# Two-layer decoder trunk on one core: partial sums moved ahead of the first evaluations, a transposition of x placed later and copied out by two engines

## The chip, the cores and the metric

The kernel runs on one core of one Trainium2 chip. The metric is device time in microseconds (us) of one execution. The core has a matrix engine (TensorE, PE in the profile, with its weight loads as PEld), a vector engine (VectorE, DVE), a scalar or activation engine (ScalarE, ACT), a general engine (GpSimd, POOL) and a sync engine (SyncE, SP). Each has its own instruction queue. Matmul results land in PSUM and are taken out by DVE or ACT; DMAs here are issued by SP and POOL.

## The reference

Two layers, each of three sub-layers with a normalisation before and after it. The input x is 512 tokens by 1024; all numbers are float32.

```python
for l in range(DEPTH):                       # DEPTH = 2
    gn = norm_gains[l]
    h = rms_norm(x, gn[0])
    x = x + 0.5 * rms_norm(swiglu(h, w_ffn1_gate[l], w_ffn1_up[l], w_ffn1_down[l]), gn[1])
    h = rms_norm(x, gn[2])
    ...                                      # mixer: gated recurrence and windowed attention
    x = x + rms_norm(mixed @ w_out[l], gn[3])
    h = rms_norm(x, gn[4])
    x = x + 0.5 * rms_norm(swiglu(h, w_ffn2_gate[l], w_ffn2_up[l], w_ffn2_down[l]), gn[5])

def swiglu(h, w_gate, w_up, w_down):         # hidden width 2816 = 22 blocks of 128
    return (jax.nn.silu(h @ w_gate) * (h @ w_up)) @ w_down
```

The change touches the four feed-forward stages (`swiglu` with its norms), not the mixer.

## The kernel before

**Number format.** Every float32 product is done as three matmuls in a rounded format: an operand is split into a high part (an ACT cast) and a low part (DVE: the number less its high part), and `mm3` (matmuls at L103) adds high·high, high·low and low·high.

**Weights.** `Stream` holds the weights' order as a list of items, one block of 128 x 1024 each. `split` (L191) makes an item's two parts: `whi` by an ACT cast (L219), `wlo` in one of two ways by the item's kind. Kinds "u", "b", "c" use DVE (L226). Kinds "v", "a", "d" use ACT for the negated number (L223) and then a DMA from POOL that adds the raw weight in flight (L224). Raw blocks come through four buffers of tag `w32`, loaded by SP (L187); a buffer is free again when its last reader is done. Six buffers each hold `whi` and `wlo`.

**A feed-forward stage** (`ffn`, L695). The first four of the gate and up blocks are made by `quad`, one accumulator (`acc`, five in all) for each. Then come pairs (gate, up) made by `twice`, 48 matmuls of 256 columns each, or in the very first stage by `project`. `gated` evaluates a pair: ACT's silu of the gate block (L706, into tile z), DVE's product with the up block (L707, into tile u). In the first stage `gated` first multiplies by the row factor rb (L701 to L704). With PLAIN = 4 (first stage FIRST = 6) pairs made that way, the remaining ones go through `fast` (L653).

**fast** computes a gate and an up block for both halves of the tokens with seven products instead of eight, in the manner of Strassen. A product is 12 matmuls of 256 columns. Products 1 and 2, the first two, use parts that are there already; the others use sums of quarters of the operand, `x56` and `x37`. `sums()` makes these for k and k + 4 at a time, so that four calls are needed. A call is, in the stages that are not the first (`Halves.sums`): four DVE additions (L496), four DVE operations in `quarter_sums` (L344 to L347), and two splits (ACT L294, DVE L295). In the first stage (`First.sums`) L411 scales x in place first, and three more splits follow. A call allocates eight tiles of tag s; that tag has 53 slots, and z and u of `gated` are of the same tag.

**Order.** PE runs in the order of the program (`manual_schedule`). For the other engines the framework's list scheduler decides the order ahead of time, with the place in the program as priority; on the chip each queue runs in the order it was given. Side work of PE is interleaved by hand: `Order` keeps a planned clock `order.t` that each matmul advances by an assumed cost, and generators (`spawn`) yield the planned ns until their next step. `order.poll()`, after each block of a matmul group, runs what is due; `order.until(cond)` runs the side work that is due next, back to back, until the condition holds.

**lay** (L394) is one such generator: it transposes x into `x_all`, 8 groups of four PE transposes (L110) through PSUM tiles of tag `aux` (three in all), each copied out by ACT (L401). It is due `WAIT["lay"]` after the start of the planned clock's side work, with `WAIT["laid"]` between groups. The first stage waits for it with `order.until(lambda: pre.laid)` after its sixth projection, since the sums overwrite x. `finish` makes rb, `gain_rows` lays out the gains; both are generators too.

Of the kernel before, what the change touches and what calls it, by code (L numbers as in the profile page):

```python
# [29 lines left out]
SLOTS = 53  # L30

WAIT = dict(
    early=0.0, first=0.0, spread=2750.0, squares=1700.0, lay=30000.0, laid=1000.0, normed=6300.0, final=2600.0,
    head=2600.0, diag=500.0, level=3000.0, chunks=1700.0, blocks=1200.0, norm=4500.0, gate=4500.0,
    values=1200.0, scores=1500.0, exp=16000.0, turn=1600.0, out=1500.0, pair=4000.0, att0=1260.0, att1=10800.0,
)
# [5 lines left out]
def trunk(ctx: ExitStack, tc: tile.TileContext, xin, wall, gains, lbT, hgain, sinks, c_dist, c_mask, c_ident, out):  # L42
    nc = tc.nc
# [15 lines left out]
    def big(dt=F32, shape=None):  # L59
        return sb.tile(shape or [P, S], dt, tag="s", name=nm("s"), bufs=SLOTS)  # L60
# [4 lines left out]
    def acc():  # L65
        return ps.tile([P, S], F32, tag="acc", name=nm("acc"), bufs=5)

    def aux():
        return ps.tile([P, S], F32, tag="aux", name=nm("aux"), bufs=3)
# [39 lines left out]
    def transpose(o, src):  # L109
        nc.tensor.transpose(o, src, ident)  # L110
        order.t += 107.0
# [3 lines left out]
    xt = [[x_all[:, t, h * S : (h + 1) * S] for h in range(2)] for t in range(TT)]  # L115
# [11 lines left out]
    p = aux()  # L127
# [144 lines left out]
    ws = Stream()  # L272
# [7 lines left out]
    def wmm(o, b, mv, start, stop, poll=True):  # L280

        mm3(o, b[2:], mv, start, stop)
        ws.used(b)
        if poll:
            order.poll()
# [76 lines left out]
    class First(Quarters):  # L362
# [31 lines left out]
        def lay(self):  # L394

            for t in range(TT):
                for h in range(2):
                    p = aux()
                    for k in range(4):
                        transpose(p[:, k * P : (k + 1) * P], xs[4 * h + k][:, t * P : (t + 1) * P])  # L400
                    nc.scalar.copy(xt[t][h], p)  # L401
                    yield WAIT["laid"]
            self.laid = True

# [200 lines left out]
    def of_half(pre, k, half):  # L605
        h = pre.h[k]
        if isinstance(pre, Halves):
            return [h[half][:, i, :] for i in range(2)]
        return h if half is None else cut(h, HALF[half])

    def quad(pre, halves):

        o = [acc() for _ in range(4)]
        blocks = {}
        ws.pinned = halves
        for half in (0, 1) if halves else (None,):
            c = WHOLE if half is None else HALF[half]
            for k in range(KT):
                order.until(lambda: pre.have[half or 0] > k)
                for j in range(4):  # L620
                    if (k, j) not in blocks:
                        blocks[k, j] = ws.next(uses=2 if halves else 1)
                    wmm(o[j][:, c], blocks[k, j], of_half(pre, k, half), k == 0, k == KT - 1)
            ws.pinned = False
        return o

    def twice(pre):

        o = acc()
        blocks = [ws.next(uses=2) for _ in range(KT)]  # L630
        for half in (0, 1):
            for k in range(KT):
                wmm(o[:, HALF[half]], blocks[k], of_half(pre, k, half), k == 0, k == KT - 1)
        return o

    def project(pre):
        o = acc()
        for k in range(KT):
            wmm(o, ws.next(), pre.h[k], k == 0, k == KT - 1)
        return o  # L640
# [12 lines left out]
    def fast(pre, a, start):  # L653

        def product(o, it, c, n):
            for k in range(4):
                wmm(o, ws.block(it, c + k), X[n][k], k == 0, k == 3)

        X = {n: pre.operand(n) for n in range(1, 8)}
        H2 = S // 2
        for j in range(start, FT):
            p1, p26, p57, p43 = acc()[:, :H2], acc(), acc(), aux()
            s, v, z = big()[:, :H2], big(F32, [P, 2, H2]), big(F32, [P, 2, H2])

            m = sb.tile([P, 4, H2], F32, tag="m", name=nm("m"), bufs=1)
            w = ws.whole()
            product(p1, w, 0, 1)
            nc.scalar.copy(s, p1)  # L670
            product(p26[:, :H2], w, 4, 2)
            if j == FT - 1:
                for i in range(EARLY):
                    a[i] = split(a[i])
            w = ws.whole()
            product(p57[:, :H2], w, 0, 5)
            product(p57[:, H2:], w, 4, 7)
            c = ws.whole()
            product(p26[:, H2:], c, 0, 6)
            pairs = [p.rearrange("p (i t) -> p i t", i=2) for p in (p26, p57, p43)]  # L680

            nc.vector.tensor_tensor(m[:, 0:4:2, :], pairs[0], s.unsqueeze(1).to_broadcast([P, 2, H2]), op=ALU.add)

            nc.vector.tensor_tensor(v, pairs[1], m[:, 2:3, :].to_broadcast([P, 2, H2]), op=ALU.add)
            w = ws.whole()
            product(p43[:, H2:], w, 4, 3)
            product(p43[:, :H2], c, 4, 4)

            nc.vector.tensor_tensor(m[:, 3, :], p57[:, :H2], v[:, 1, :], op=ALU.add)
            nc.vector.tensor_tensor(m[:, 1:3, :], pairs[2], v[:, ::-1, :], op=ALU.add)  # L690
            nc.scalar.activation(out=m[:, 0:2, :], in_=m[:, 0:2, :], func=AF.Silu)
            nc.vector.scalar_tensor_tensor(z, m[:, 0:2, :], -1.0, m[:, 2:4, :], op0=ALU.mult, op1=ALU.mult)
            a.append(z.rearrange("p i t -> p (i t)"))

    def ffn(l, n, pre, nxt, halves=True):  # L695
        a = []

        def gated(og, ou):
            z, u = big(), big()
            if first:  # L700
                nc.vector.tensor_tensor(z, og, pre.rb, op=ALU.mult)  # L701
                nc.scalar.activation(out=z, in_=z, func=AF.Silu)
                nc.vector.tensor_tensor(u, ou, pre.rb, op=ALU.mult)
                nc.vector.tensor_tensor(u, u, z, op=ALU.mult)  # L704
            else:
                nc.scalar.activation(out=z, in_=og, func=AF.Silu)  # L706
                nc.vector.tensor_tensor(u, ou, z, op=ALU.mult)  # L707
            a.append(u)

        first = isinstance(pre, First)  # L710
        o = quad(pre, halves)
        if first:
            o.append(project(pre))
            order.until(lambda: pre.rb is not None)
        for j in range(2):
            gated(o[2 * j], o[2 * j + 1])
        if first:
            gated(o[4], project(pre))
            order.until(lambda: pre.laid)
            for j in range(3, FIRST):  # L720
                for _ in range(2 if j == 5 else 1):
                    pre.sums()
                gated(project(pre), project(pre))
            fast(pre, a, FIRST)
        else:
            for j in range(2, PLAIN):
                gated(twice(pre), twice(pre))
                pre.sums()
                pre.sums()
            fast(pre, a, PLAIN)  # L730
        return down(a, FT, l, n + 1, nxt)

# [309 lines left out]
    for l in range(DEPTH):  # L1042
        for n in (0, 2, 4):
            if n == 2:
                ws.plain((4 * H + 4 + 2 + 2 * KT) * KT // 8 + 2 * KT * 4 // 8)
                ws.rows(KT)
            else:
                p = FIRST if l + n == 0 else PLAIN
                ws.plain(6)
                ws.plain(2 * p - 6, "v" if l + n == 0 else "u")  # L1050
                ws.pairs(FT - p)
                ws.rows(FT)
    pre = First()
# [65 lines left out]
    for l in range(DEPTH):  # L1119
        pre = ffn(l, 0, pre, (l, 2), halves=l > 0)  # L1120
        pre = mixer(l, pre, (l, 4))
        pre = ffn(l, 4, pre, (l + 1, 0) if l + 1 < DEPTH else None)
# [81 lines left out]
```

## Time and profile before

| | |
|---|---|
| runs | 2213.29, 2214.19, 2214.93 us; median 2214.19 |
| profiled execution | 2213.53 us, span 2211.8 us |
| busy | PE 2172.0, DVE 1366.2, ACT 1046.4, POOL 125.9 us |
| mean granted clock of PE | 0.991 |
| HBM read, written | 200.99 MB, 2.15 MB |

The span is the time from the first to the last instruction that the profile records; the execution's own time is 1.7 us longer. A name such as "L294" is a line of the kernel; "s<-acc" means that a tile of tag s is written from one of tag acc; "x8" is a count. A row of the timeline has start, length, engine, line, operation, tiles, count, and in brackets how long the engine stood idle before it and what released it. Matmul rows overlap, so that the distance of their starts is what counts.

The four feed-forward stages begin, roughly, at 0, 742, 1104 and 1840 us; the first mixer lies between the first and the second of them, the second mixer between the third and the fourth.

### The profile page before, as it was taken

How to read it: one execution, taken by the hardware profiler on the slowest of the kernel's cores; microseconds unless marked ns; L12 is line 12 of the kernel's file. 1: busy time of each engine (PE TensorE's matmuls, PEld its weight loads, DVE VectorE, ACT ScalarE, POOL GpSimd, SP SyncE). 2: the span in 40 equal slices, each digit the busy share in tenths (PEclk: the TensorE clock that was granted, in tenths of full speed). 3: DMA queues.
4: the chain of work that ended last, by engine and by line, in shares of the span. 5: the costliest groups of instructions: out<-in, count | busy, mean ns of one | idle time of the engine just before them, and what ended most of it. 6: DMA issues, size and time to landing. Idle time of an engine off the chain costs nothing.

```text
span 2211.8 us, 34593 instructions
## 1 busy us (share of the span) xinstructions
PE 2172.0 (98%) x13625; PEld 1958.7 (89%) x13625; DVE 1366.2 (62%) x2375; ACT 1046.4 (47%) x1709; POOL 125.9 (6%) x150
## 2 busy tenths in 40 slices
PE   9999999999999989999999999999999999899998
PEld 7999988878888989998899998898788889899987
DVE  5778725756633667883476786267565437777823
ACT  7555515455423545562445555253543335455612
POOL 0111000000000011100001110000000000111000
PEclk9999999999999999999999999999999999999999
DMA  8577532212233238773236775322112322578631
GB/s 241 125 180 185 169 99 74 86 58 66 69 101 99 87 92 185 183 200 96 76 101 148 177 185 163 95 86 67 58 58 86 96 96 77 118 178 186 188 94 39
DMA packets 126419, 263.60 MB, mean 119 GB/s; under 512 B 13392, under 2 KB 71216, under 8 KB 126256
## 3 DMA queue, kind: packets, MB, share of 16 engines
q1 hardware_dynamic: 105088, 203.13, 29.1%
q0 software_dynamic: 21024, 58.21, 15.2%
q8 instruction: 107, 1.75, 0.3%
q14 instruction: 56, 0.46, 0.1%
q10 hardware_dynamic: 144, 0.05, 0.0%
HBM read 200.99 MB, written 2.15 MB: 92 GB/s over the span
## 4 chain that ended last, share of the span: by engine, by line
PE 93%; DVE 4%; DMA 1%; ACT 1%; issue 1%; SPq 0%; DVEq 0%; ACTq 0%; POOLq 0%
PE acc L103 68%; PE aux L103 23%; PE aux L110 1%; DMA w<-wall 1%; PE acc L110 1%; DVE wlo L226 0%; DVE s L496 0%; DVE s L295 0%; DVE s L768 0%; DMA s<-xin 0%; DVE s L453 0%; DVE s L937 0%; ACT whi L219 0%; DMA wlo<-w 0%; DMA g_sb<-gains 0%
## 5 line engine op out<-in xcount | busy, mean ns | idle before, releaser
L103 PE MATMUL acc<-s,whi 128*128 128x256 f32 (+1 forms) x5104 | 1106.2, 313 | 23.7 <-ACT s L294 16.3
L103 PEld LDWEIGHTS acc<-s,whi 128*128 128x128 f32 x5104 | 839.0, 192 | 73.2 <-ACT s L294 17.8
L103 PE MATMUL acc<-s,wlo 128*128 128x256 f32 (+1 forms) x2552 | 794.2, 311 | 0.1
L219 ACT CAST whi<-w 128x1024 fp32r<-128x1024 f32 (+1 forms) x373 | 360.7, 969 | 673.0 <-PE aux L103 276.8
L226 DVE TENSOR_TENSOR wlo<-w,whi 128x1024 fp32r<-128x1024 f32 (+1 forms) x227 | 276.1, 1218 | 407.8 <-ACT whi L219 403.9
L103 PEld LDWEIGHTS acc<-s,wlo 128*128 128x128 f32 x2552 | 490.6, 192 | 26.3 <-DVE wlo L226 0.4
L103 PE MATMUL acc<-whi,s 128*128 128x512 f32 x1296 | 424.2, 393 | 0.0
L103 PEld LDWEIGHTS acc<-whi,s 128*128 128x128 f32 x1296 | 243.3, 188 | 50.9
L103 PE MATMUL acc<-wlo,s 128*128 128x512 f32 x648 | 252.5, 390 | 0.0
L224 POOL DMA_DIRECT2D wlo<-w x146 | 125.7, 861 | 1942.7 <-ACT wlo L223 1790.1
L103 PE MATMUL aux<-whi,s 128*128 128x512 f32 x624 | 207.8, 390 | 0.0
L103 PE MATMUL aux<-s,whi 128*128 128x256 f32 x1120 | 204.6, 283 | 0.0
L226 DVE TENSOR_TENSOR wlo<-tt,whi 128x1024 fp32r<-128x1024 f32 x140 | 170.5, 1218 | 12.8 <-ACT whi L219 12.7
L103 PEld LDWEIGHTS aux<-s,whi 128*128 128x128 f32 x1120 | 174.7, 192 | 0.0
L219 ACT CAST whi<-tt 128x1024 fp32r<-128x1024 f32 x140 | 145.8, 1041 | 31.0 <-PE acc L103 20.8
L103 PE MATMUL aux<-s,wlo 128*128 128x256 f32 x560 | 158.5, 283 | 0.0
L103 PEld LDWEIGHTS acc<-wlo,s 128*128 128x128 f32 x648 | 121.8, 188 | 23.8
L103 PEld LDWEIGHTS aux<-whi,s 128*128 128x128 f32 x624 | 117.2, 188 | 24.1
L206 DVE TENSOR_TENSOR tt<-w,w 128x512 f32<-128x512 f32 x70 | 48.4, 691 | 133.4 <-DMA w<-wall 118.4
L223 ACT ACTIVATE wlo<-w 128x1024 fp32r<-128x1024 f32 (+1 forms) x146 | 124.1, 850 | 0.0
L103 PE MATMUL aux<-wlo,s 128*128 128x512 f32 x312 | 121.4, 389 | 0.0
L103 PEld LDWEIGHTS aux<-s,wlo 128*128 128x128 f32 x560 | 107.5, 192 | 0.0
(163 smaller groups left out, 1889.0 us busy)
## 6 DMA issues: line engine op xcount, KB each, us to landing
w<-wall SPq DMA_DIRECT2D x283, 512.0 KB, 3.5
w<-wall SPq DMA_DIRECT2D x352, 128.0 KB, 2.6
wlo<-w POOLq DMA_DIRECT2D x76, 512.0 KB, 5.9
wlo<-w POOLq DMA_DIRECT2D x70, 256.0 KB, 4.2
grow<-rows_d SPq DMA_DIRECT2D x6, 512.0 KB, 5.0
s<-xin SPq DMA_DIRECT2D x8, 256.0 KB, 6.5
y<-s SPq DMA_DIRECT2D x8, 256.0 KB, 2.5
w<-wall SPq DMA_DIRECT2D x2, 256.0 KB, 4.3
```

The source lines that it names most:

```text
L103: nc.tensor.matmul(o, lhsT, rhs, start=start, stop=stop)
L110: nc.tensor.transpose(o, src, ident)
L206: nc.vector.tensor_tensor(self.t13[:, h[0]], w[:, h[0]], v[:, h[0]], op=ALU.add)
L219: i = nc.scalar.copy(it.hi[:, c], w[:, c])
L223: nc.scalar.mul(it.lo[:, c], w[:, c], -1.0)
L224: nc.gpsimd.dma_start(it.lo[:, c].bitcast(F32), w[:, c], accum_op=ALU.add)
L226: nc.vector.tensor_tensor(it.lo[:, c], w[:, c], it.hi[:, c].bitcast(F32), op=ALU.subtract)
```

## The change

Four edits. In the stages that are not the first, two calls of `sums()` stand ahead of the first `gated`, one ahead of each of the two following pairs; before, two followed each of these pairs. `lay` becomes due at 32000 instead of 30000 planned ns, with 1500 instead of 1000 between groups. Its copies alternate between ACT (h = 0) and DVE (h = 1). In the list of weights, the first eight blocks instead of six of each feed-forward stage are of kind "u"; the remaining ones among the plain blocks are "v". As the stages with PLAIN = 4 have eight plain blocks, all "u" before too, this alters two blocks of the first stage only.

```diff
-    early=0.0, first=0.0, spread=2750.0, squares=1700.0, lay=30000.0, laid=1000.0, normed=6300.0, final=2600.0,
+    early=0.0, first=0.0, spread=2750.0, squares=1700.0, lay=32000.0, laid=1500.0, normed=6300.0, final=2600.0,
...
                     for k in range(4):
                         transpose(p[:, k * P : (k + 1) * P], xs[4 * h + k][:, t * P : (t + 1) * P])
-                    nc.scalar.copy(xt[t][h], p)
+                    (nc.vector.tensor_copy if h else nc.scalar.copy)(xt[t][h], p)
                     yield WAIT["laid"]
...
             o.append(project(pre))
             order.until(lambda: pre.rb is not None)
+        if not first:
+            pre.sums()
+            pre.sums()
         for j in range(2):
             gated(o[2 * j], o[2 * j + 1])
...
             for j in range(2, PLAIN):
+                if j < 4:
+                    pre.sums()
                 gated(twice(pre), twice(pre))
-                pre.sums()
-                pre.sums()
             fast(pre, a, PLAIN)
...
                 p = FIRST if l + n == 0 else PLAIN
-                ws.plain(6)
-                ws.plain(2 * p - 6, "v" if l + n == 0 else "u")
+                ws.plain(8)
+                ws.plain(2 * p - 8, "v")
                 ws.pairs(FT - p)
                 ws.rows(FT)
```

## Prediction

> **What bounds the kernel now.** I read the busy times first, then what TensorE (PE) waited for, then the matmuls around the longest waits, and last the queues of VectorE (DVE) and ScalarE (ACT) at those places. The first line is from the page, the others from the list of waits of PE; there the columns are us in total, times, longest.
>
> ```profile
> PE 2172.0 (98%) x13625; PEld 1958.7 (89%) x13625; DVE 1366.2 (62%) x2375; ACT 1046.4 (47%) x1709; POOL 125.9 (6%) x150
> PE acc L103 <- ACT s L294: 16.3, 6, 4.1
> PE acc L103 <- DVE s L295: 5.8, 6, 1.6
> PE aux L110 <- ACT x_all L401: 2.5, 2, 1.7
> ```
>
> PE is busy for 98% of the span, so only two things can shorten it: fewer waits, or fewer matmuls at a lowered clock. The two longest waits are for L294 and L295, the ACT cast and the DVE subtraction that end each `sums()`. They come six times each, two in each of the three feed-forward stages that are not the first; the third, 2.5 us, is for `lay` (L401) in the first stage.
>
> The stage table prices the three. The rows are, for the stage at 742 us, the stretch before `fast`, its first product group (j=4) and its second; then the first group of the other two stages. The columns are length, then busy time of PE, PEld, DVE, ACT, POOL, then PE's clock, DMA share, GB/s.
>
> ```profile
> 751.43:790.32 38.89, 38.89 (x326) 38.89 (x326) 24.20 (x44) 17.13 (x26) 2.58 (x3) 1.00 0.43 114
> 790.32:810.97 20.65, 13.30 (x86) 12.32 (x86) 15.03 (x30) 7.42 (x11) 0.86 (x1) 0.75 0.18 42
> 810.97:821.05 10.08, 10.08 (x86) 10.08 (x86) 8.05 (x11) 5.94 (x9) 1.72 (x2) 1.00 0.68 171
> 1151.76:1172.57 20.81, 13.47 (x86) 12.48 (x86) 15.03 (x30) 7.42 (x11) 0.86 (x1) 0.75 0.17 41
> 1888.65:1909.63 20.98, 13.54 (x86) 12.55 (x86) 15.03 (x30) 7.42 (x11) 0.86 (x1) 0.76 0.12 31
> ```
>
> A group is 7 products of 12 matmuls, 84 in all, and takes 10.08 us (0.12 us a matmul). The first of each stage takes 20.65, 20.81 and 20.98 us. Just before, 38.89 us pass without a PE gap. So each stage loses 10.57, 10.73 and 10.90 us there: 32.2 us. About 7.3 of each is waiting (16.3 + 5.8 over three); the remaining 3.3 is matmuls at a granted clock of 0.75 instead of 1.00 and short gaps.
>
> Why are the sums late? DVE's order in the stage at 742 us, from the timeline (start, length):
>
> ```profile
> 752.88 2.43 DVE L484 SCALAR_TENSOR_TENSOR s<-aux,g_sb,s 128x256 fp32r<-128x256 f32 x6
> 768.25 0.69 DVE L707 TENSOR_TENSOR s<-acc,s 128x512 f32<-128x512 f32 x1 [4.52 <-ACT s L706]
> 770.92 0.68 DVE L206 TENSOR_TENSOR tt<-w,w 128x512 f32<-128x512 f32 x1
> 778.89 0.69 DVE L707 TENSOR_TENSOR s<-acc,s 128x512 f32<-128x512 f32 x1 [2.15 <-PE acc L103]
> 779.50 1.42 DVE L496 TENSOR_TENSOR s<-s 128x256 f32<-128x256 f32 x4
> 783.95 1.42 DVE L496 TENSOR_TENSOR s<-s 128x256 f32<-128x256 f32 x4
> 790.41 0.69 DVE L707 TENSOR_TENSOR s<-acc,s 128x512 f32<-128x512 f32 x1 [1.93 <-PE acc L103]
> 791.02 1.42 DVE L496 TENSOR_TENSOR s<-s 128x256 f32<-128x256 f32 x4
> 798.38 1.42 DVE L496 TENSOR_TENSOR s<-s 128x256 f32<-128x256 f32 x4
> 802.26 1.51 DVE L295 TENSOR_TENSOR s<-s,s 128x512 fp32r<-128x512 f32 x2
> ```
>
> Two sums follow the third evaluation (L707 at 778.89) at once, two the fourth (790.41). The last pair thus starts when PE is already at `fast`, and its last L295 runs at 802.26, 12 us after PE began the group. Yet the inputs (L484, 752.88 + 2.43) were there at 755.3. What holds a sum is not the data but its place: its tiles have the tag s, as those of the evaluations before it, and L206, which has other tiles and stands still later in the program, ran at 770.92, ahead of it. I conclude that tiles of one tag are given out in program order. This is an inference from the order of the rows.
>
> **The change part by part.**
>
> *Sums moved, three stages.* Nothing is added: four sums before, four after (12 in the kernel), with the same instructions and no DMA; no queue of SP or POOL is passed. Two now stand ahead of the first evaluation, one after the second, one after the third. The first two can start at 755.3. A sum takes 783.95 − 779.50 = 4.45 us of DVE, two 8.9. These rows show the first two evaluations on ACT and the rest of a sum:
>
> ```profile
> 767.62 0.60 ACT L706 ACTIVATE s<-acc 128x512 f32<-128x512 f32 x1
> 782.08 1.14 ACT L294 CAST s<-s 128x512 fp32r<-128x512 f32 x2 [2.19 <-DVE s L345]
> 786.54 1.14 ACT L294 CAST s<-s 128x512 fp32r<-128x512 f32 x2
> L226 DVE TENSOR_TENSOR wlo<-w,whi 128x1024 fp32r<-128x1024 f32 x3 | 3.7, 1223 | 1.7 <-ACT whi L219 1.7
> ```
>
> From 755.3 to L707 at 768.25 are 12.9 us; in them DVE does two L226 (1.22 each; the last row is DVE's groups over the 752 to 767.4 window) and four additions of the L206 kind (0.69), 5.2 us, so 7.7 are free. Two sums end near 769.5, about 1.3 us later than L707 now starts. Who waits? L707 frees an accumulator; there are five, and the one that the second `twice` takes at about 773.2 (767.4, when the quad is done, and 48 matmuls of 0.12) is freed by ACT's L706 at 767.62 + 0.60 = 768.2. The casts of the second sum stand ahead of it on ACT, and end at about 768: L706 slips by under 1 us against a slack of 5. Cost nothing; the cover is that slack. The third sum follows the second evaluation, at about 771 to 776, the fourth the third, at 779.5 to 784, where the first is now: both before `fast` at 790.3. Ends: the full 32.2 us, or less where a product of the group waits on something else. Next in line are the weights of the group. Their last casts come before or within the old stall; I take the full 32.2, since the second group runs at 10.08 us right behind the stall.
>
> *Two blocks of the first stage from "v" to "u".* Two L223 leave ACT, two L224 leave POOL, two L226 join DVE.
>
> ```profile
> L223 ACT ACTIVATE wlo<-w 128x1024 fp32r<-128x1024 f32 (+1 forms) x146 | 124.1, 850 | 0.0
> 33.42 0.18 DVE L330 RECIPROCAL rc<-rc 128x4 f32<-128x4 f32 x1 [6.37 <-ACT rc L329]
> 26.43 4.66 DMA wlo<-w
> 31.15 7.82 DMA w<-wall
> ```
>
> DVE gains 2 x 1.22 us in a place where it sat idle for 6.37; ACT loses two L223 of 0.85 on the mean. The last two rows, from the chain, show the other side: a raw buffer is released only when the accumulating DMA has read it, and the next load follows at 31.15. Through DVE the two loads can start some 3 us sooner (4.66 of DMA and POOL's issue against one L226). No wait of PE for these blocks is in the list above, so I set the edit itself at 0; if DVE's idle place were gone it would cost 2.4 us of DVE. What it gives is a sooner load for the next edit.
>
> *lay later and evacuated by both engines.* The planner's clock decides. A 512-column matmul counts 213.3, an fp32 one four times as much. At the end of the quad the clock stands at 3200 (15 warm-up matmuls of 213.3) + 96 x 213.3 = 23680, after the next projection (24 x 213.3) and the two steps of `finish` (432 and 853) at 30085, and after the sixth projection at 35205. `lay` now falls due at 33200, inside this projection; four groups go between its products and four in a row behind it. With 32000 it is due at 35200, so that all eight go in a row from the projection's last product on.
>
> ```profile
> 41.32 0.60 PE L110 MATMUL aux<-ident,s 128*128 128x128 f32 x4
> 47.06 1.14 PE L110 MATMUL aux<-ident,s 128*128 128x128 f32 x8 [1.74 <-ACT x_all L401]
> 48.98 1.83 PE L110 MATMUL aux<-ident,s 128*128 128x128 f32 x8 [0.78 <-ACT x_all L401]
> 50.46 1.20 PE L103 MATMUL acc<-s,whi 128*128 128x512 f32 x2
> 44.55 1.28 ACT L1095 ACT_TABLE_LOAD   x1
> 45.45 0.69 DVE L206 TENSOR_TENSOR tt<-w,w 128x512 f32<-128x512 f32 x1 [1.78 <-DMA w<-wall]
> L558 DVE COPY s<-acc 128x512 f32<-128x512 f32 x4 | 2.8, 692 | 4.9 <-PE acc L110 4.8
> 50.00:60.00 10.00, 10.00 (x42) 8.31 (x41) 9.93 (x23) 7.46 (x11) 1.54 (x2) 0.87 0.48 106
> ```
>
> From 41.32 to 50.46, PE did 8 groups (0.45 us each) and three products (0.68 each), 5.6 us of work in 9.1: 3.5 lost, and some 0.8 more on slow first matmuls after it. That 4.3 us is the most this edit can give. The eight copies were one engine's; four go to DVE at 0.69 us (L558 is a copy of that shape) instead of ACT's 0.59. With 3 aux buffers, the burst is paced by PE (3.6 us) if both engines are free. The other end: ACT's table load (1.28) and DVE's L206, which waits for a load and would have copies queued behind it, hold the burst as they do now and now have eight groups to hold: up to 3 us worse. The loads come sooner, so I stand nearer the good end: −2.0 us, ends −4.3 and +3.
>
> *A rule on the clock.* The 50 to 60 slice has clock 0.87 although no wait ahead of it exceeds 1.74 us. The Trainium skill (TensorE: Matmul & The Clock Gate, "What's actually happening") says that the clock halves only after an idle window of about 3.4 us. By that rule the short waits of `lay` would cost no clock, and this edit could give only the 3.5 us. The trace does not agree, unless several short waits fill one window. The sum stays as it is.
>
> **Sum.** −32.2 − 2.0 = −34.2 us against the profiled execution's 2213.53 us (span 2211.8, 1.7 around it): 2179.3. The median of the runs is 2214.19, 0.7 above, so I say 2180.
>
> **The rivals.**
>
> *A: the early sums hold the queues.* If the first two sums don't get DVE before the quad ends (767.4), their casts end 787.68 − 779.50 = 8.2 us later, 775.6, and L706 behind them on ACT, at 776.2, frees the accumulator 3.0 us too late. With 1.4 us of slow clock (now 3.3 us for 7.3 of waiting, taken in proportion) that is 4.4 a stage, 13.2 in all: 2213.5 − 32.2 + 13.2 − 2 = 2192.5. For it: ACT and DVE work in order in every row shown. Against: the data are there at 755.3 and 7.7 us are free. The Trainium skill (TensorE: Matmul & The Clock Gate, "Architectural detail") calls both queues strictly first in, first out, which is the mechanism of this rival; the trace agrees, as with L206's wait of 1.78 us at 45.45.
>
> *B: the weights take the stall's place.* Loads and casts were made ready during the stall. If half of it came back as waits on them, the time would be 2213.5 − 16.1 − 2 = 2195.4. Against: second groups have 10.08 us with the DMA at 0.68, and the stall's window moved only 42 GB/s.
>
> *C: the sums stay where they are,* because something other than the order of tiles holds them. Only the first stage changes: 2211.5 to 2214, no measurable difference.
>
> *D, slower: the sums run late and stand ahead of everything.* If their tiles came free only where the first sum gets them now, 779.50, L706 would come at 787.7 and the second `twice`, due at 773.2, would stand for 14.5 us, plus at least the 3.3 of slow clock of now. Against the 10.7 saved that is +7.1 a stage, 21.3 in all: 2213.5 + 21.3 − 2 = 2232.8. The stage turns slower once wait and slow clock pass 10.7, that is a wait of 7.4 us or casts that end after about 780. Against: between L484 and the first evaluation no other tile of the tag is given out.
>
> **How the numbers follow.** Forecast 0.74, A 0.11, B 0.05, C 0.06, D 0.04. The forecast's own range is 2175 (all of `lay`'s 4.3 and some more of slow clock) to 2186 (`lay` 3 worse, and up to 1 us left in each stage). A and half of B lie below 2195; with them the range is 2175 to 2195, and C, D and the rest of B stay out, somewhat over 1 in 10. A change under 0.2% (4.4 us) can hardly be told from none here. Faster by more: forecast, A and B, 0.90; within: C, 0.06; slower: D, 0.04.
>
> **What the next profile would show.** Right: two runs of L496 between L484 and the first L706 of each of the three stages, the others before the fourth evaluation; no wait of PE for L294 or L295; the first group at 10.1 us and clock 1.00; L223 at 144, L401 split 4 and 4 between ACT and DVE; one run of 32 transposes near 43 us, shorter than the 9.1 us of now. Wrong: a wait of PE ahead of the second `twice` for L706 or L707 (A, D), for whi or wlo in the first groups (B), or L496 still behind the third L707 (C).

## The result, and the profile after

| | before | after |
|---|---|---|
| median of four runs each | 2213.76 us | 2179.2 us (2178.42 to 2180.1) |
| ratio after to before | | 0.9843, 95% interval 0.9826 to 0.986 |
| profiled execution, span | 2213.53, 2211.8 us | 2179.35, 2177.6 us |

The change made the kernel faster by 1.6%, and the span shorter by 34.2 us. The first two lines are from the page of the kernel after, the others from the list of waits of PE (us in total, times, longest):

```profile
PE 2161.6 (99%) x13625; PEld 1951.4 (90%) x13625; DVE 1369.7 (63%) x2381; ACT 1043.5 (48%) x1703; POOL 124.2 (6%) x148
L223 ACT ACTIVATE wlo<-w 128x1024 fp32r<-128x1024 f32 (+1 forms) x144 | 122.0, 847 | 0.0
PE acc L110 <- DVE x_all L570: 2.5, 1, 2.5
PE aux L103 <- DVE s L295: 1.5, 2, 0.7
PE aux L110 <- DVE x_all L401: 0.7, 1, 0.7
PE aux L110 <- ACT x_all L401: 0.2, 1, 0.2
```

PE does the same 13625 matmuls. The waits of `acc` for L294 and L295, 22.1 us before, are gone; the L295 that is left belongs to `aux` in the mixer and has the same 1.5 us in the other profiles. The wait for `lay`'s copies fell from 2.5 to 0.9 us. The stage table, with the columns of the prediction's; the first two rows are the stage at 742 us, up to `fast` and in `fast`'s first group, the next two the first groups of the two other stages, the last a slice of the first stage:

```profile
747.77:786.66 38.89, 38.89 (x326) 38.89 (x326) 31.30 (x64) 19.41 (x30) 2.58 (x3) 1.00 0.42 110
786.66:796.74 10.08, 10.08 (x86) 10.08 (x86) 7.63 (x10) 5.07 (x7) 0.86 (x1) 1.00 0.44 99
1137.51:1147.59 10.08, 10.08 (x86) 10.08 (x86) 7.63 (x10) 5.07 (x7) 0.86 (x1) 1.00 0.44 98
1865.11:1875.19 10.08, 10.08 (x86) 10.08 (x86) 7.63 (x10) 5.07 (x7) 0.86 (x1) 1.00 0.42 98
50.00:60.00 10.00, 10.00 (x46) 8.24 (x45) 9.64 (x20) 6.90 (x13) 0.86 (x1) 1.00 0.67 149
```

The stretch ahead of `fast` takes the same 38.89 us, now with 64 DVE operations in it instead of 44, and each first group takes 10.08 us at clock 1.00 instead of 20.65 to 20.98 us at 0.75 to 0.76.

Where the 34.2 us came from is read from the chain. Some of its pieces are long runs of matmuls: one stands near the start of each mixer (x150), one near its end (x441), and after the change one opens the following stage (x384). First before, then after:

```profile
376.51 19.94 PE acc L103 x150
601.16 99.99 PE acc L103 x441
1474.66 19.94 PE acc L103 x150
1699.49 99.99 PE acc L103 x441
```

```profile
372.90 19.94 PE acc L103 x150
597.51 99.99 PE acc L103 x441
747.77 46.08 PE acc L103 x384
1449.67 19.94 PE acc L103 x150
1675.93 100.01 PE acc L103 x441
```

| stretch | before | after | difference |
|---|---|---|---|
| start to first mixer (first stage) | 376.51 | 372.90 | −3.61 |
| first mixer, x150 to x441 | 224.65 | 224.61 | −0.04 |
| to the second mixer (two stages) | 873.50 | 852.16 | −21.34 |
| second mixer, x150 to x441 | 224.83 | 226.26 | +1.43 |
| to the end (last stage) | 512.31 | 501.67 | −10.64 |

The x441 run itself counts to the row below it. The 1.43 us given back in the second mixer, which the change doesn't touch, are taken up under the hardware below.

### The profile page after: what moved, and what is told of

Read it like the earlier page. It is cut to its first block, busy times and chain, and to the rows that moved or that the text cites. A ratio compares the mean times of both kernels' runs of the same rounds, so it can differ in the third digit from the quotient of the medians.

```text
span 2177.6 us, 34576 instructions
## 1 busy us (share of the span) xinstructions
PE 2161.6 (99%) x13625; PEld 1951.4 (90%) x13625; DVE 1369.7 (63%) x2381; ACT 1043.5 (48%) x1703; POOL 124.2 (6%) x148
## 4 chain that ended last, share of the span: by engine, by line
PE 95%; DVE 2%; DMA 1%; ACT 1%; issue 1%; SPq 0%; POOL 0%; DVEq 0%; POOLq 0%; ACTq 0%
PE acc L103 70%; PE aux L103 23%; PE aux L110 1%; DMA w<-wall 1%; PE acc L110 1%; DMA s<-xin 0%; DVE s L453 0%; DMA wlo<-w 0%; DVE s L940 0%; DVE wlo L226 0%; DVE s L771 0%; DMA g_sb<-gains 0%; DVE s L566 0%; ACT s L509 0%; DVE s L576 0%
## 5 line engine op out<-in xcount | busy, mean ns | idle before, releaser
L206 DVE TENSOR_TENSOR tt<-w,w 128x512 f32<-128x512 f32 x70 | 48.4, 691 | 126.8 <-DMA w<-wall 116.9
```

Of the source, the lines that this page charges most:

```text
L206: nc.vector.tensor_tensor(self.t13[:, h[0]], w[:, h[0]], v[:, h[0]], op=ALU.add)
```

## The experiments

Each ratio is of the kernel named to the kernel before, run on the same chip, with its 95% interval.

### The sums alone

The kernel before with the moved sums and none of the other edits:

```diff
+        if not first:
+            pre.sums()
+            pre.sums()
...
+                if j < 4:
+                    pre.sums()
                 gated(twice(pre), twice(pre))
-                pre.sums()
-                pre.sums()
```

> The kernel before with the sums moved and nothing else. Theory (the whole gain of the three later stages is the stall at the first product group of fast, and it vanishes): the first groups take 10.1 us at clock 1.00, no wait of PE for L294 or L295, 30.6 to 32.2 us less than before, 2181 to 2183 us. Rival (the move only shifts the wait, and part of the gain came from the first stage's edits or from sooner loads): a wait of some us is left in each stage, 2190 us or more.

2184.12 us (2181.41 to 2187.68), ratio 0.9866 (0.9851 to 0.9881): 31.2 us less than the runs of before beside it, and a little above the 2181 to 2183 expected. The profiled span is 2179.6, 32.2 less than before's, with the first mixer at 376.83, close to where before has it (376.51). No wait of `acc` for L294 or L295 is left. So the term of the sum that was worked out from the stage table is what the chip gives.

### The other edits alone

The kernel after with the sums where they were before:

> The changed kernel with the sums back in their old place: only the first stage's edits (lay later and alternately copied, two blocks by DVE). Theory: the three stalls stay at 20.6 to 21.0 us a first group, the first stage ends 3.6 us sooner, 2210 us. Rival (the first stage's gain needs the moved sums, or is given back behind it): 2212 to 2214 us, no difference that can be told.

2210.86 us (2208.47 to 2212.94), ratio 0.9978 (0.9969 to 0.9987). The waits of PE are those of before:

```profile
PE acc L103 <- ACT s L294: 16.8, 6, 4.3
PE acc L103 <- DVE s L295: 5.9, 6, 1.6
```

The first mixer starts at 373.15, 3.4 us sooner than before. The two halves of the change add up: by the medians they gain 31.2 and 4.4 us alone and 34.6 us together, which agrees within the spread of the runs.

### Another tag instead of another place

Was it the place in the program that held the sums, by tiles of one tag being given out in order? Here the sums stay where before has them, and the evaluations' tiles get a tag of their own (z and u are one tile then, as four buffers are all that room is left for):

```diff
-SLOTS = 53
+SLOTS = 49
...
-            z, u = big(), big()
+            if first:
+                z, u = big(), big()
+            else:
+                z = u = sb.tile([P, S], F32, tag="g", name=nm("g"), bufs=4)
```

> The kernel before with its sums where they are in the program; only z and u of gated, in the stages that are not the first, become one tile of a tag of their own (four slots; the tag s has 49 instead of 53). Theory (tiles of one tag are given out in program order, and that alone held the sums): L496 runs ahead of the first evaluation although it stands behind the third in the program, the stalls vanish, 2181 to 2183 us. Rival (the place in the program holds them, or their data): L496 stays behind the third L707, 2213 us.

2181.73 us (2181.56 to 2185.27), ratio 0.9853 (0.984 to 0.9867): the whole gain of the sums, without moving them. In DVE's timeline the evaluation's product is L710 in this kernel:

```profile
755.71 0.41 DVE L496 TENSOR_TENSOR s<-s 128x256 f32<-128x256 f32 x1
758.46 1.09 DVE L496 TENSOR_TENSOR s<-s 128x256 f32<-128x256 f32 x3
765.49 1.42 DVE L496 TENSOR_TENSOR s<-s 128x256 f32<-128x256 f32 x4
768.73 1.29 DVE L710 TENSOR_TENSOR g<-acc,g 128x512 f32<-128x512 f32 x2 [0.22 <-ACT g L709]
```

Though the program has three calls of `gated` ahead of the first sum, two sums now run ahead of the first product. The sums' data were there all along; the shared tag held them.

### Four sums ahead

Rivals A and D: the same sums, too early. All four stand ahead of the first evaluation:

```diff
-            pre.sums()
-            pre.sums()
+            for _ in range(4):
+                pre.sums()
...
-                if j < 4:
-                    pre.sums()
```

> The changed kernel with all four sums ahead of the first evaluation. Theory (both queues run in order and the slack at the second twice is about 5 us, rival A of the prediction): the last casts end near 774 us on the scale of the changed kernel's second stage, the silu that frees the accumulator comes behind them, the second twice, due near 769.5, waits 4 to 6 us and then runs on a lower clock for 2 to 3 us; 6 to 9 us a stage, 2197 to 2206 us. Rival (the sums' place ahead of the evaluations costs nothing however many they are): 2179 to 2181 us.

2215.29 us (2213.44 to 2216.37), ratio 1.0003 (0.9994 to 1.0012). The gain is gone, and more than was expected is lost. Waits of PE, the queue of ACT, PE's restart, and the window around it (columns as in the stage table):

```profile
PE acc L103 <- ACT s L706: 30.5, 3, 10.2
776.76 1.14 ACT L294 CAST s<-s 128x512 fp32r<-128x512 f32 x2 [5.01 <-DVE s L345]
777.91 1.28 ACT L706 ACT_TABLE_LOAD   x1
779.21 1.57 ACT L706 ACTIVATE s<-acc 128x512 f32<-128x512 f32 x3
779.86 0.80 PE L103 MATMUL acc<-s,whi 128*128 128x256 f32 x2 [10.17 <-ACT s L706]
769.70:790.00 20.30, 10.14 (x63) 10.14 (x64) 10.72 (x21) 7.20 (x11) 0.13 (x1) 0.66 0.05 20
```

The fourth sum's casts end at 777.90; a table load and the silus wait behind them; the second `twice` waits 10.17 us for an accumulator and then runs slow, at 0.66 over the 20 us. The expectation had the last casts end near 774 and a wait of 4 to 6 us. The first additions of the sums came at 751.90, 760.37, 766.79 and 773.69, that is 6.4 to 8.5 us apart and not 4.45, as DVE also does the split of weights between them. The casts 3.9 us later than expected and the table load (1.28 us) are the miss. Rival D's break-even, casts that end after about 780, is 776.7 on this kernel's clock (it reaches the stage some 3.3 us sooner). They ended 1.2 later, and from the last L484 to the first L690, behind the first group, the three stages took 59.3 to 60.6 us instead of before's 58.1 to 58.5. So the time equals before's although the first stage is faster.

### No sum ahead of the first evaluations

In place of two sums ahead of the first, all come in pairs behind the second and the third:

```diff
-        if not first:
-            pre.sums()
-            pre.sums()
...
-                if j < 4:
+                for _ in range(2):
                     pre.sums()
```

> The changed kernel with two sums right behind the first two evaluations and two behind the third: one place earlier than before, none ahead of the first evaluation. Theory (a sum takes 6.9 us of the clock when weights are converted between its parts, as the four sums ahead of the evaluations did, so four from 768.9 us end near 795, past the 790 at which fast needs the last): a wait of 3 to 5 us a stage with 1.5 to 2 of slow clock, 2192 to 2200 us. Rival (4.45 us a sum, as the prediction had it: the four end at 787): no wait, 2179 to 2182 us.

2177.73 us (2176.91 to 2181.03), ratio 0.9835 (0.9819 to 0.985). PE's list has no wait for a sum. The last L295 in DVE's timeline:

```profile
790.77 0.68 DVE L295 TENSOR_TENSOR s<-s,s 128x512 fp32r<-128x512 f32 x1
791.97 0.68 DVE L295 TENSOR_TENSOR s<-s,s 128x512 fp32r<-128x512 f32 x1
```

They are the fourth sum's, `x56` first and then `x37` in the program's order, and end at 791.45 and 792.65. `fast`'s first group starts at 788.59 in this kernel. Its first two products (24 matmuls of 0.12, 2.88 us) and nine matmuls of the third (1.08 us) don't need the fourth sum. The third product, n = 5, takes `x56`, which is needed at 792.55; the fourth, n = 7, takes `x37`, needed 12 matmuls later at 793.99. So they came 1.1 and 1.3 us ahead. (Product 4 uses no sum either, but comes last.) The theory of 6.9 us a sum fell: behind the quad's evaluations the sums began 5.0 to 6.8 us apart. For the time it is enough here that no sum stands behind the fourth evaluation; the two ahead of the first buy room (in the changed kernel the last L295 ends 6.2 us ahead of the group), no time that these runs can tell.

### The two weight blocks

The kernel after with six "u" blocks again:

```diff
-                ws.plain(8)
-                ws.plain(2 * p - 8, "v")
+                ws.plain(6)
+                ws.plain(2 * p - 6, "v" if l + n == 0 else "u")
```

> The changed kernel with the two blocks of the first stage back at kind v (ACT and the accumulating DMA of POOL). Theory (the prediction's: the edit by itself costs nothing, but the raw buffers come free sooner, and with them the load that DVE's L206 waits for; copies of lay now stand behind L206): without it L206 waits some 3 us longer, the burst of transposes is held for 1 to 2.5 us, 2180 to 2182 us. Rival (the edit does nothing): 2178 to 2180 us, the burst from 43.1 to 47.8 us as in the changed kernel.

2186.31 us (2183.88 to 2186.45), ratio 0.9867 (0.9849 to 0.9885). The first mixer starts at 379.89, 7.0 us later than after's and 3.1 later than with the sums alone. In the timeline, the last row a window:

```profile
40.07 1.05 ACT L219 CAST whi<-w 128x1024 fp32r<-128x1024 f32 x1 [2.96 <-DMA w<-wall]
46.78 0.69 DVE L206 TENSOR_TENSOR tt<-w,w 128x512 f32<-128x512 f32 x1 [2.12 <-DMA w<-wall]
47.65 0.21 ACT L1098 ACTIVATE lbex<-lbex 128x8 f32<-128x8 f32 x1 [1.30 <-DVE lbex L1097]
48.39 0.66 PE L110 MATMUL aux<-ident,s 128*128 128x128 f32 x4 [3.41 <-ACT x_all L401]
50.00:60.00 10.00, 9.85 (x39) 8.36 (x40) 9.32 (x28) 3.44 (x7) 0.86 (x1) 0.69 0.50 117
```

This is the prediction's bad end, and more of it than the 2180 to 2182 us expected. L206 waits for a load, and PE waits 3.41 us and then runs at 0.69. The rows show a longer path than a copy behind L206: DVE's L1097 stands behind L206, ACT's L1098 waits for L1097, and the copy that ends PE's 3.41 us stands behind L1098 on ACT. Only the next wait of PE, 1.10 us, is for a copy on DVE. With the sums alone, where ACT makes all the copies, the longest wait there is 2.14 us by the same path. So `lay`'s edits without the sooner loads cost 3.1 us, read from one profile each.

The opposite, the kernel before with eight "u" blocks and nothing else:

> The kernel before with one edit: the two blocks of the first stage by DVE (kind u). Theory (formed after the fifth run: this edit alone makes the first stage's gain, since raw buffers come free sooner and the casts, silus and L206 that stood behind a load on ACT and DVE with them): the first stage ends 3 to 5 us sooner than before, at 372 to 373 us where the first mixer's long run of matmuls begins (before 376.5), 2209 to 2211 us in all. Rival (the edit helps only the copies that the change put behind L206): the first stage ends as before, 2213 to 2215 us.

2209.53 us (2208.72 to 2211.98), ratio 0.9975 (0.9966 to 0.9984). The first mixer starts at 372.02, 4.5 us sooner than before's, and the span is 4.1 us shorter. The first row is before's, the other three this kernel's:

```profile
39.07 1.05 ACT L219 CAST whi<-w 128x1024 fp32r<-128x1024 f32 x1 [2.07 <-DMA w<-wall]
36.46 1.05 ACT L219 CAST whi<-w 128x1024 fp32r<-128x1024 f32 x1
41.82 0.69 DVE L206 TENSOR_TENSOR tt<-w,w 128x512 f32<-128x512 f32 x1 [0.67 <-DMA w<-wall]
46.07 1.15 PE L110 MATMUL aux<-ident,s 128*128 128x128 f32 x8 [0.31 <-ACT x_all L401]
```

The cast that stood idle for a load until 39.07 in the kernel before runs at 36.46 without a wait, L206 comes at 41.82 instead of 45.45, and `lay`'s copies wait for less. What held the loads is in the waits of SP, which issues them. Between 20 and 45 us, five loads of the kernel before wait for an accumulating DMA to be done with a raw buffer (22.6 us in all); here three do (16.9 us). Two blocks that leave the accumulating DMA are the whole gain of the first stage.

### lay's two edits

ACT alone copying, and the due time as before, each in the kernel after:

```diff
-                    (nc.vector.tensor_copy if h else nc.scalar.copy)(xt[t][h], p)
+                    nc.scalar.copy(xt[t][h], p)
```

> The changed kernel with all eight copies of lay on ACT again. Theory (the burst is paced by the engines that copy, and ACT has a cast of 1.05 us and a table load between its copies): the first matmul behind the burst comes 1 to 2.5 us later than 47.84, 2180 to 2182 us. Rival (PE paces the burst, the second engine is not needed): 2178 to 2180 us.

```diff
-    ... lay=32000.0, laid=1500.0, ...
+    ... lay=30000.0, laid=1000.0, ...
```

> The changed kernel with lay due at 30000 and 1000 planned ns as before; copies alternate, blocks as changed. Theory (what held the groups of before was ACT's load of a table and DVE's wait at L206, not the place alone; both are milder now): about half of the first stage's 3.6 us is lost, 2180 to 2181.5 us. Rival (the place is the whole gain of the first stage): 2182 to 2183 us.

With ACT alone: 2177.35 us (2176.27 to 2179.63), ratio 0.9832 (0.9816 to 0.9847), first mixer at 371.82, 1.1 us sooner than with both engines. The theory's 2180 to 2182 us fell, and the rival's reading holds. PE does all eight groups in one run, with no idle time in it:

```profile
43.13 3.89 PE L110 MATMUL aux<-ident,s 128*128 128x128 f32 x32
```

The copies are not what paces the burst, and a second engine only puts half of them behind other work on DVE: in the changed kernel the burst came in three pieces, with waits of 0.65 and 0.24 us. With the old due time: 2177.36 us (2177.03 to 2180.48), ratio 0.9833 (0.9818 to 0.9849), first mixer at 373.09, within 0.2 us of after's. The place is worth nothing; both numbers expected for it were too high.

Both undone together, that is the moved sums and the two blocks alone:

> The sums moved and the two blocks by DVE, with lay wholly as before (due at 30000 and 1000, copies by ACT alone). Theory (lay's own edits give nothing once the loads come sooner): 2176 to 2179 us, not slower than the changed kernel. Rival (both are needed): 2180 to 2182 us.

2178.35 us (2176.47 to 2179.89), ratio 0.9832 (0.9819 to 0.9846), first mixer at 372.05. Nothing of `lay`'s edits is needed.

### One pair fewer ahead of fast

A try at a better version: ACT copies, and PLAIN = 3, so that one more pair goes through `fast`, whose group has 84 matmuls instead of 96 of 256 columns (12 by 0.12 = 1.44 us a stage, 4.3 in three). The list of weights follows with six plain blocks a stage:

```diff
-W32, WS, AHEAD, TAIL, PLAIN, FIRST, EARLY = 4, 6, 3, 2, 4, 6, 4
+W32, WS, AHEAD, TAIL, PLAIN, FIRST, EARLY = 4, 6, 3, 2, 3, 6, 4
...
-                if j < 4:
+                for _ in range(2):
                     pre.sums()
```

> The changed kernel with lay's copies on ACT alone, and with PLAIN = 3: one plain pair less and one more pair by fast in each of the three later stages, 96 matmuls replaced by 84 (1.44 us a stage); two sums ahead of the first evaluation, two behind the second. Theory (the deadline of the last sum, now 12 us away from its need in the changed kernel at most, moves 11.5 us nearer, and DVE has 29 us of work from 751.6 to 779.5): a wait of 1 to 4 us with some slow clock in each stage eats the gain, 2177 to 2187 us. Rival (the sums still fit): 2173 to 2174 us.

2179.45 us (2177.75 to 2180.97), ratio 0.9839 (0.9825 to 0.9852): no better. Waits of PE:

```profile
PE acc L110 <- DVE s L576: 2.3, 3, 1.2
PE acc L103 <- DVE s L295: 1.9, 3, 0.6
```

Of the 4.3 us, 4.2 come back as two waits: the last sum is late again by 0.6 us a stage, and the stage's start waits up to 1.2 us for a normalisation (L576). That stands on DVE behind an L206, which in the stage at 742 us waits 0.65 us for its load.

### The changed kernel again

> The changed kernel once more. Theory (the 1.6 us that one mixer passage of it lost to a lowered clock depends on the execution and not on the program): 2177 to 2181 us, each of its two mixer passages either 224.7 or 226.3 us from the first to the last of their long runs of matmuls, not the same one slow by necessity. Rival (the program's order makes it): again 224.6 and 226.3.

2177.69 us (2176.95 to 2179.78), ratio 0.9832 (0.9819 to 0.9846); span 2175.2, with mixer passages of 224.62 and 224.74 us. So the changed kernel, ACT copies, the old due time, no sum ahead, and sums with two blocks cannot be told apart by their times.

## Why the prediction was right, and where only its sum was

**Sums, −32.2 us: right, by the right steps.** The sums alone took 32.2 us off the span, and after's stages gained 10.6 to 10.7 each. That a shared tag held them (rival C's question) was inferred from row order and is now shown by the own tag. That the weights don't take the stall's place (rival B) is shown by three first groups at 10.08.

**Its sub-step "L706 slips by under 1 us": wrong, but covered.** DVE and ACT in the stage at 742 us of the kernel after:

```profile
751.58 1.42 DVE L496 TENSOR_TENSOR s<-s 128x256 f32<-128x256 f32 x4
760.05 1.42 DVE L496 TENSOR_TENSOR s<-s 128x256 f32<-128x256 f32 x4
764.59 0.62 ACT L294 CAST s<-s 128x512 fp32r<-128x512 f32 x1
765.22 1.28 ACT L706 ACT_TABLE_LOAD   x1
766.52 1.09 ACT L706 ACTIVATE s<-acc 128x512 f32<-128x512 f32 x2
768.86 1.42 DVE L496 TENSOR_TENSOR s<-s 128x256 f32<-128x256 f32 x4
775.91 1.42 DVE L496 TENSOR_TENSOR s<-s 128x256 f32<-128x256 f32 x4
779.14 1.29 DVE L295 TENSOR_TENSOR s<-s,s 128x512 fp32r<-128x512 f32 x2 [0.23 <-ACT s L294]
```

The first two sums lie 8.5 us apart, not 4.45. L706 starts 18.75 us after the quad's start (766.52 − 747.77) against 16.19 before: it slipped by 2.6 us. Half of that is the table load of 1.28 us, which the prediction's path left out: before, it ran ahead of the quad's end (766.32), and now it stands behind the casts. As the slack was 5.0, PE didn't wait. The four-ahead kernel shows how near the edge is: two more sums there, and the same path costs 10.17 us a stage. Rival A named the right mechanism; its 4.4 us was for two late sums, and the margin held with 2.4 us left. Rival D's 14.5 us is counted to the start of L706, where rival A counts to its end, 0.6 us later; nothing hangs on it.

**Two blocks, 0 us: the term that was mis-sized.** It measured −4.5 us up to the first mixer (−4.1 in the span). The argument, that PE waits for no such block, looked only at the blocks' own consumers. The prediction itself had the mechanism, loads some 3 us sooner (the cast came 2.6 us sooner, 39.07 to 36.46), and L206's wait for a load with the copies behind it, but booked its effect under `lay`. That the raw buffers set the time of the loads is what the waits of SP show.

**lay, −2.0 us: the other half of the same error.** The burst did shrink, from 41.32 to 50.46 with three products in it to 43.08 to 47.84. But the blocks alone shorten it as well. Beside them, `lay`'s edits measured +0.9 (372.90 against 372.05), or +0.4 in the repeat (372.46), which the copies on DVE (1.1) can account for; without the blocks they measured +3.1, the predicted bad end. The two wrong terms partly cancel: predicted together −2.0, measured −3.6.

**The sum −34.2 us: partly luck.** It was hit to the tenth, since the first stage's extra 1.6 us and the second mixer's 1.4 us given back cancel out. In the repeat, where the mixers gave nothing back, the span is 36.6 us shorter than before's. Four runs of either program lie within 1.7 us here, the repeat's within 2.8, and 21 runs of before beside the first experiments within 7.5 (2211.75 to 2219.29), so that no more than a few us of agreement should be read into it.

**The clock rule.** The slice at 50 us, 0.87 before after waits of at most 1.74 us, is at 1.00 where the waits are 0.7 and 0.2, and at 0.69 after one of 3.41. All 14 traces say the same of this burst. From 50 to 52 us the clock is 0.50 to 0.55 in the four whose longest wait there is 1.74 (before), 2.14 (the sums alone), 2.83 (own tag) and 3.41 us (six "u" blocks), and 1.00 in the ten whose longest is 1.38 us or less. So short waits did go with a lower clock here, as the sum assumed; PE had only transposes between them, and no run separates the two. The Trainium skill (TensorE: Matmul & The Clock Gate, "What's actually happening") asks for an idle window of about 3.4 us before the clock halves; the drops after 10.17 and 3.41 us agree with it, those after 1.74 to 2.83 us and the one below do not as it is worded.

## What to carry to other kernels

When an engine does something late although its inputs are long there, look at which tiles it allocates: a tag shared with work that waits can hold it, and either a tag of its own or another place in the program frees it. How early to put such work is bounded on both sides, by its consumer and by what queues behind it on each engine; price it with all the work that runs between its parts, not with its own durations. And an edit to how a block is made should be priced by when it releases its buffer, not only by who waits for the block.

## What the runs showed of the hardware

The length of a mixer passage differs between executions of the same program. In 26 passages (both mixers of before, after, and all experiments but the four-ahead one, whose chain doesn't show the runs) 19 took 224.6 to 224.9 us and 7 took 226.2 to 226.5. The changed kernel's second passage belonged to the 7 in one profile and to the 19 in the repeat. The two windows stand at the same instructions, after and then its repeat, with the columns of the stage table:

```profile
1556.92:1560.26 3.34, 3.34 (x11) 2.66 (x12) 3.14 (x7) 0.59 (x1) 0.00 (x0) 0.53 0.02 5
```

```profile
1556.48:1559.97 3.49, 3.49 (x20) 2.96 (x20) 3.45 (x8) 1.99 (x3) 0.00 (x0) 1.00 0.02 5
```

In both, PE had idled just before for the same short times (0.73 and 0.28 us after, 0.75 and 0.28 in the repeat), and in one of them the clock was 0.53 for some 3.3 us, 11 matmuls in place of 20. The Trainium skill (TensorE: Matmul & The Clock Gate, "What's actually happening") says that the window in which activity is judged runs freely, so that the number of slow matmuls at a kernel's start varies from run to run. The variation here is of that kind but lies in the middle of a kernel; no run here shows the window itself, and why waits this short can be enough stays open. For this kernel it means steps of about 1.6 us a passage. Two such steps would cover the 2.8 us between the repeat's runs, but the passages are known for the profiled runs alone.
